# Three of seven quarter products with an operand's high and low parts side by side in one matmul

## The chip, the cores and the metric

The kernel runs on one core of one Trainium2 chip. The metric is device time in microseconds of one execution; lower is better. Before the change three runs took 1763.12 to 1763.74 us, median 1763.62. A core has a matrix engine (TensorE, PE in the profile; its weight loads are PEld), VectorE (DVE), ScalarE (ACT), GpSimd (POOL) and a queue engine (SP) that issues transfers. Matmul results land in PSUM, which this kernel uses as eight banks of 512 float32 columns.

## The reference

A decoder trunk of two layers over 512 tokens of width 1024, in float32. Each layer has a feed-forward block, a mixer, a second feed-forward block and a norm:

```python
h = x + 0.5 * swiglu(rms_norm(x, ffn1_norm[l]), ffn1_w1[l], ffn1_w3[l], ffn1_w2[l])
...
h = h + y @ w_out[l]          # y: convolution, sliding-window attention, memory attention
h = h + 0.5 * swiglu(rms_norm(h, ffn2_norm[l]), ffn2_w1[l], ffn2_w3[l], ffn2_w2[l])
x = rms_norm(h, final_norm[l])

def swiglu(x, w1, w3, w2):
    return (jax.nn.silu(x @ w1) * (x @ w3)) @ w2
```

The inner width is 2816, so 22 blocks of 128 columns of w1 and w3. The change is in the products with w1 and w3.

## The kernel before

**Precision.** A float32 operand is cut into a high part (ScalarE copies it to the matmul's rounded type) and a low part (VectorE subtracts the high part, L147). Three matmuls make one product: high x high, high weight x low data, low weight x high data (`mm3`, L178 to L180).

**Feed-forward.** `ffn` takes the first four of the 22 blocks plainly, as 512-column matmuls. The other 18 are taken in 9 pairs by `up_pair`. There each 2x2 product of halves (two blocks of weight columns by two halves of the 1024 channels, times two halves of the channels by two halves of the tokens) is formed from seven products of quarters instead of eight: sums and differences of weights (`wsum`, `raw`) times sums and differences of data. Each quarter product has 256 token columns and four blocks of 128 channels, so 12 matmuls. A pair does this for w1 (into `u`) and w3 (into `g`), 14 products in all, 168 matmuls.

**The data operands.** `Seven` holds the seven data operands as high and low parts: `first` makes those of products 1, 2 and 6 in the tiles `mh` and `ml`, `rest` those of 3, 5, 7 and 4 in `xhi` and `xlo`. Sums of quarters are VectorE adds (`msum`). They are made once per feed-forward block, while the four plain blocks and the first pairs run.

**Results.** Products accumulate in PSUM banks named after their pool: `po` (two), `pt` (two), `mm` (three) and `cf` (one). In a pair, products 1, 2, 6 and 5 used one `po` bank per weight (`xy`), 3, 7 and 4 one `pt` bank per weight (`zv`). ScalarE copies some results to SBUF (`part`), VectorE adds the rest (`add`, L386).

**Order.** The program is written once; a scheduler sets the order on each engine, and each engine then runs its own list in that order. The weight tiles `whi` and `wlo` have four buffers, `raw` and `aux` three. Each engine waits on semaphores at the head of its list, so whatever stands behind a waiting instruction waits too. The products with w2 (`begin` in `ffn`, 512 columns, `mm`) come after a group of pairs and may be mixed with its last products.

Of the kernel before, what the change touches and what calls it, by code (L numbers as in the profile page):

```python
# [11 lines left out]
F32R = mybir.dt.float32r  # L12
I32 = mybir.dt.int32
AF = mybir.ActivationFunctionType
ALU = mybir.AluOpType
AX = mybir.AxisListType
ALL = slice(None)

P = 128
D = 1024  # L20
S = 512
# [44 lines left out]
def trunk(ctx: ExitStack, tc: tile.TileContext, xT, memT, pos, w1a, w3a, w2a, w1b, w3b, w2b,  # L66
          wconv, wqk, wvm, wmem, wout, gains, small, rows, consts, out):
    nc = tc.nc
    V, G, A, T = nc.vector, nc.gpsimd, nc.scalar, nc.tensor

    const = ctx.enter_context(tc.tile_pool(name="const", bufs=1))
    res = ctx.enter_context(tc.tile_pool(name="res", bufs=1))
# [7 lines left out]
    turn, tail, hold = [0], [None], {}  # L80
# [10 lines left out]
    def bank(shape, tag):  # L91

        if tag == "mm":
            return ps_mm.tile(shape, F32, tag=tag, name=tag)
        return ps_ax.tile(shape, F32, tag=tag, name=tag, bufs=1 if tag == "cf" else 2)

    def tm(name, tag="t", bufs=None):
        return tmp.tile([P, S], F32, tag=tag, name=name, **({"bufs": bufs} if bufs else {}))
# [4 lines left out]
    def raw_tile(src, cols):  # L103
        raw = wst.tile([P, UNIT], F32, tag="raw", name="raw", bufs=3)
        nc.sync.dma_start(raw[:, 0:cols], src)
        return raw
# [5 lines left out]
    first = []  # L112
# [32 lines left out]
    def split(hi, lo, x, on):  # L145
        a = A.activation(hi, x, AF.Copy)  # L146
        return a, on.tensor_tensor(out=lo, in0=x, in1=hi.bitcast(F32), op=ALU.subtract)  # L147
# [29 lines left out]
    def mm3(ps, a, b, first, last, **more):  # L177
        T.matmul(ps, a[0], b[0], start=first, stop=False, **more)  # L178
        T.matmul(ps, a[0], b[1], start=False, stop=False, **more)  # L179
        tail[0] = T.matmul(ps, a[1], b[0], start=False, stop=last, **more)  # L180

    def at(p, *idx):
        return tuple(x[idx] for x in p)

    def blk(k, n=P):
        return slice(k * n, (k + 1) * n)
# [57 lines left out]
    class Stat:  # L244


        def __init__(self, tag, n=S, on=None):
            self.sums, self.tag, self.n, self.on = [], tag, n, on
# [18 lines left out]
    def operand():  # L267
        return (res.tile([P, KD, S], F32R, tag="xhi", name="xhi"), res.tile([P, KD, S], F32R, tag="xlo", name="xlo"))
# [16 lines left out]
    QT = 256  # L285
# [9 lines left out]
    class Seven:  # L295


        def __init__(self, n):
            self.n = n
            self.m = {}  # L300

        def quarter(self, half, i, t):

            return self.n[2 * half + i][:, :, blk(t, QT)]

        def first(self):
            near = (res.tile([P, 3, 4, QT], F32R, tag="nsh", name="mh"), res.tile([P, 3, 4, QT], F32R, tag="nsl", name="ml"))
            for i, j in enumerate((1, 2, 6)):
                self.m[j] = at(near, ALL, i)
            self.plain(1, 0, 0)  # L310
            self.plain(2, 1, 0)
            f = self.sum((0, 1), (1, 1), ALU.subtract)
            self.sum(f, (0, 0), ALU.subtract, f)
            self.cut(6, f)
# [7 lines left out]
            return out  # L322

        def plain(self, j, half, t):
            for i in range(2):
                hi, lo = at(self.m[j], ALL, blk(i, 2))
                split(hi, lo, self.quarter(half, i, t), V)

        def cut(self, j, f):
            hi, lo = (x.rearrange("p k t -> p (k t)") for x in self.m[j])  # L330
            split(hi, lo, f, V)

        def rest(self):
            far = tuple(x.rearrange("p k (u t) -> p (k u) t", t=QT) for x in operand())
            for i, j in enumerate((3, 5, 7, 4)):
                self.m[j] = at(far, ALL, blk(i, 4))
            self.plain(3, 1, 1)
            self.cut(5, self.sum((0, 0), (0, 1), ALU.subtract))
            f = self.sum((1, 1), (0, 1), ALU.subtract)
            self.cut(7, f)  # L340
            self.sum(f, (0, 0), ALU.add, f)
            self.sum(f, (1, 0), ALU.subtract, f)
            self.cut(4, f)
# [5 lines left out]
    def gated():  # L349
        p = gated_pair()  # L350
        return [at(p, ALL, i, ALL) for i in range(2)]

    def unit(x):
        p = pair()
        split(p[0], p[1], x, V)
        return p

    def up_pair(l, w13, f, M):

        raw = [raw_tile(w13[i][l, f], D) for i in range(2)]  # L360
        X = []
        for i in range(2):

            x = wst.tile([P, UNIT], F32, tag="aux", name="wsum", bufs=3)
            nc.sync.dma_start(x.rearrange("p (f c) -> p f c", f=2), w13[i][l, f : f + 2, :, 0:QW].rearrange("f p c -> p f c"))
            G.dma_start(x, w13[i][l, f + 1], accum_op=ALU.add)
            X.append(x)
        z = wst.tile([P, UNIT], F32, tag="raw", name="raw", bufs=3)
        for i in range(2):
            nc.sync.dma_start(z[:, blk(i, QW)], w13[i][l, f + 1, :, QW:])  # L370
        xy = [bank([P, S], "po") for _ in range(2)]
        zv = [bank([P, S], "pt") for _ in range(2)]
        x0, x1 = blk(0, QT), blk(1, QT)

        def product(ps, w, half, j, first=False):


            for k in range(4):
                mm3(ps, at(w, ALL, blk(4 * half + k)), at(M.m[j], ALL, k), first and k == 0, k == 3, skip_group_check=True)

        u, g = (tmp.tile([P, 2, S], F32, tag=t, name=t, bufs=n) for t, n in (("u", 1), ("g", 2)))
        part = [tm("part", "sq", 2) for _ in range(2)]
        to = (u, g)

        def add(out, a, b):
            V.tensor_tensor(out=out, in0=a, in1=b, op=ALU.add)  # L386

        for i in range(2):
            w = unit(raw[i])
            product(xy[i][:, x0], w, 0, 1, first=True)  # L390
            product(xy[i][:, x1], w, 1, 2)
            A.activation(part[i], xy[i], AF.Copy)
            add(to[i][:, 0, x0], part[i][:, x0], part[i][:, x1])

            add(raw[i][:, 0:QW], raw[i][:, 0:QW], X[i][:, QW:])
            add(raw[i][:, QW:], raw[i][:, QW:], raw[i][:, 0:QW])
        for i in range(2):
            w = unit(raw[i])
            product(xy[i][:, x0], w, 0, 6)
            A.activation(part[i][:, x1], xy[i][:, x0], AF.Copy)  # L400
            product(zv[i][:, x0], w, 1, 3, first=True)
        for i in range(2):
            w = unit(X[i])
            product(xy[i][:, x0], w, 1, 5)
            A.activation(part[i][:, x0], xy[i][:, x0], AF.Copy)
            product(zv[i][:, x1], w, 0, 7)
            add(to[i][:, :, x1], zv[i].rearrange("p (n t) -> p n t", n=2), part[i][:, x0].unsqueeze(1).to_broadcast([P, 2, QT]))
        w = unit(z)
        for i in range(2):
            product(zv[i][:, x1], w, i, 4)  # L410
            add(to[i][:, 1, x0], zv[i][:, x1], part[i][:, x1])
        out = gated()
        for n, sign in enumerate((1.0, -1.0)):
            A.activation(u[:, n], u[:, n], AF.Silu, scale=sign)
        M.gated = V.tensor_tensor(out=g, in0=g, in1=u, op=ALU.mult)
        for n, sign in enumerate((1.0, -1.0)):
            hi, lo = out[n]
            A.activation(hi, g[:, n], AF.Copy, scale=sign)
            V.scalar_tensor_tensor(out=lo, in0=g[:, n], scalar=sign, in1=hi.bitcast(F32), op0=ALU.mult, op1=ALU.subtract)
        return out  # L420

    def ffn(l, w13, w2, x, sums, factors, last, at_product, aside=None, closing=None):
# [55 lines left out]
        for q, (f0, nf) in enumerate(QUARTERS):  # L478
            ahead = 2 if q + 1 < len(QUARTERS) else 0
            for f in range(f0, f0 + nf + ahead, 2):  # L480
                if f not in g:
                    g[f], g[f + 1] = up_pair(l, w13, f, M)
                    if f == PLAIN:
                        with tc.issue_after(M.gated.ins):
                            rescale = after()
# [615 lines left out]
    for l in range(L):  # L1101
        x, new = nxt.x, Stat("st")
# [163 lines left out]
```

## Time and profile before

| | |
|---|---|
| three runs | 1763.12 to 1763.74 us, median 1763.62 |
| the profiled execution | 1764.53 us, its span 1762.8 us |
| granted TensorE clock | 0.998 |
| TensorE busy | 1746.5 us, 11004 matmuls |
| VectorE busy | 1281.3 us, 1898 instructions |
| ScalarE busy | 900.7 us, 1373 instructions |
| GpSimd busy | 195.6 us, 220 instructions |
| from HBM | 249.67 MB |

Times in the profile are microseconds from the start of the span. A timeline row is: start, duration, engine, line, operation, output<-inputs by the program's names, shapes; in square brackets the idle time just ahead of it and what ended that. Group rows have count, busy time, mean nanoseconds, idle time. Matmuls overlap, and their ends are modelled, so their starts tell more than their durations.

### The profile page before, as it was taken

How to read it: one execution, taken by the hardware profiler on the slowest of the kernel's cores; microseconds unless marked ns; L12 is line 12 of the kernel's file. 1: busy time of each engine (PE TensorE's matmuls, PEld its weight loads, DVE VectorE, ACT ScalarE, POOL GpSimd, SP SyncE). 2: the span in 40 equal slices, each digit the busy share in tenths (PEclk: the TensorE clock that was granted, in tenths of full speed). 3: DMA queues.
4: the chain of work that ended last, by engine and by line, in shares of the span. 5: the costliest groups of instructions: out<-in, count | busy, mean ns of one | idle time of the engine just before them, and what ended most of it. 6: DMA issues, size and time to landing. Idle time of an engine off the chain costs nothing.

```text
span 1762.8 us, 28084 instructions
## 1 busy us (share of the span) xinstructions
PE 1746.5 (99%) x11004; PEld 1576.7 (89%) x11004; DVE 1281.3 (73%) x1898; ACT 900.7 (51%) x1373; POOL 195.6 (11%) x220
## 2 busy tenths in 40 slices
PE   8999999999999999999999999999999999999998
PEld 7989999988888989898889898989888889998987
DVE  7968666589877757575677786666898677665756
ACT  6646444355765535353655463444467654353533
POOL 1001000006121000000010010000251310000000
PEclk9999999999999999999999999999999999999999
DMA  9456645257257546465567465642671766474622
GB/s 285 120 162 171 181 133 149 65 159 177 72 105 170 146 140 170 131 166 140 155 139 183 129 181 142 168 132 79 164 172 36 155 144 166 134 185 116 169 81 84
DMA packets 97205, 253.60 MB, mean 144 GB/s; under 512 B 9904, under 2 KB 16304, under 8 KB 97072
## 3 DMA queue, kind: packets, MB, share of 16 engines
q1 hardware_dynamic: 78064, 190.45, 35.4%
q0 software_dynamic: 19008, 61.35, 19.4%
q8 instruction: 86, 1.41, 0.3%
q14 instruction: 47, 0.39, 0.1%
HBM read 249.67 MB, written 2.10 MB: 143 GB/s over the span
## 4 chain that ended last, share of the span: by engine, by line
PE 98%; DVE 1%; DMA 1%; ACT 0%; issue 0%; SPq 0%; DVEq 0%; ACTq 0%
PE mm L178 14%; PE mm L179 14%; PE mm L180 14%; PE po L178 9%; PE po L179 9%; PE po L180 9%; PE pt L178 6%; PE pt L179 6%; PE pt L180 6%; PE po L870 2%; PE mm L818 1%; PE cf L178 1%; PE cf L180 1%; PE cf L179 1%; PE pt L859 1%; DMA raw<-in_w2b 1%
## 5 line engine op out<-in xcount | busy, mean ns | idle before, releaser
L146 ACT ACTIVATE whi<-raw 128x1024 fp32r<-128x1024 f32 (+3 forms) x346 | 326.2, 946 | 440.9 <-PE mm L179 219.9
L147 DVE TENSOR_TENSOR wlo<-raw,whi 128x1024 fp32r<-128x1024 f32 (+3 forms) x346 | 376.0, 1088 | 118.9 <-ACT whi L146 118.0
L179 PE MATMUL mm<-glo,whi 128*128 128x512 f32 (+1 forms) x752 | 292.1, 388 | 0.0
L178 PE MATMUL mm<-ghi,whi 128*128 128x512 f32 (+1 forms) x752 | 291.8, 390 | 0.0
L180 PE MATMUL mm<-ghi,wlo 128*128 128x512 f32 (+1 forms) x734 | 284.9, 388 | 0.0
L178 PE MATMUL pt<-xhi,whi 128*128 128x256 f32 x864 | 243.3, 283 | 1.4 <-DVE g L386 1.4
L180 PE MATMUL po<-mh,wlo 128*128 128x256 f32 x864 | 244.5, 283 | 0.0
L179 PE MATMUL po<-ml,whi 128*128 128x256 f32 x864 | 244.5, 283 | 0.0
L178 PE MATMUL po<-mh,whi 128*128 128x256 f32 x864 | 244.4, 283 | 0.0
L180 PE MATMUL pt<-xhi,wlo 128*128 128x256 f32 x864 | 243.9, 283 | 0.0
L179 PE MATMUL pt<-xlo,whi 128*128 128x256 f32 x864 | 243.9, 283 | 0.0
L506 DVE SCALAR_TENSOR_TENSOR h<-mm,h 128x512 f32<-128x512 f32 x126 | 86.3, 688 | 132.0 <-PE mm L180 131.9
L178 PEld LDWEIGHTS pt<-xhi,whi 128*128 128x128 f32 x864 | 165.2, 192 | 2.4 <-DVE g L386 1.6
L178 PEld LDWEIGHTS mm<-ghi,whi 128*128 128x128 f32 x752 | 141.4, 188 | 28.8 <-DVE h L506 1.2
L179 PEld LDWEIGHTS pt<-xlo,whi 128*128 128x128 f32 x864 | 165.7, 192 | 0.8
L178 PEld LDWEIGHTS po<-mh,whi 128*128 128x128 f32 x864 | 165.8, 192 | 0.7
L179 PEld LDWEIGHTS po<-ml,whi 128*128 128x128 f32 x864 | 165.8, 192 | 0.6
L179 PEld LDWEIGHTS mm<-glo,whi 128*128 128x128 f32 x752 | 141.3, 188 | 27.5
L180 PEld LDWEIGHTS po<-mh,wlo 128*128 128x128 f32 x864 | 165.8, 192 | 0.0
L180 PEld LDWEIGHTS pt<-xhi,wlo 128*128 128x128 f32 x864 | 165.7, 192 | 0.0
L180 PEld LDWEIGHTS mm<-ghi,wlo 128*128 128x128 f32 x734 | 137.8, 188 | 28.5
L1000 DVE SCALAR_TENSOR_TENSOR there<-ypad,par,there 128x512 f32<-128x512 f32 x180 | 136.0, 779 | 1.3
(334 smaller groups left out, 3322.0 us busy)
## 6 DMA issues: line engine op xcount, KB each, us to landing
raw<-in_w2a SPq DMA_DIRECT2D x48, 384.0 KB, 3.5
raw<-in_w2b SPq DMA_DIRECT2D x48, 384.0 KB, 3.6
raw<-in_w1b SPq DMA_DIRECT2D x26, 512.0 KB, 3.6
raw<-in_w3b SPq DMA_DIRECT2D x26, 512.0 KB, 3.7
raw<-in_w1a SPq DMA_DIRECT2D x25, 512.0 KB, 3.6
raw<-in_w3a SPq DMA_DIRECT2D x25, 512.0 KB, 4.0
wsum<-in_w1a SPq DMA_DIRECT2D x18, 512.0 KB, 4.4
wsum<-in_w3a SPq DMA_DIRECT2D x18, 512.0 KB, 4.3
```

The source lines that it names most:

```text
L146: a = A.activation(hi, x, AF.Copy)
L147: return a, on.tensor_tensor(out=lo, in0=x, in1=hi.bitcast(F32), op=ALU.subtract)
L178: T.matmul(ps, a[0], b[0], start=first, stop=False, **more)
L179: T.matmul(ps, a[0], b[1], start=False, stop=False, **more)
L180: tail[0] = T.matmul(ps, a[1], b[0], start=False, stop=last, **more)
L506: added = V.scalar_tensor_tensor(out=h[:, d, :], in0=ps, scalar=0.5, in1=h[:, d, :], op0=ALU.mult, op1=ALU.add)
L818: tail[0] = T.matmul(pp[i][:, z, :], q, k, start=not masked, stop=True, skip_group_check=True)
L859: tail[0] = T.transpose(pt[:, i, j, :], pr[:, i, blk(j)], ident)
L870: tail[0] = T.matmul(po[:, 2 * c + i, :], ptb[:, i, j, :], v, start=(j == 0), stop=(j == nk - 1))
L1000: V.scalar_tensor_tensor(out=cv[:, c, :], in0=ypad[:, c, j : j + S], scalar=conv_w[:, c, j : j + 1], in1=cv[:, c, :], op0=ALU.mult, op1=AL ...
```

## The change

An operand's high and low parts now lie beside each other, 256 columns each, for every block of channels. In products 2, 7 and 4 (`beside`) one matmul of 512 columns takes the high weight part times both, into the two halves of a bank; the low weight part times the high data part is added to the first half by a matmul of 256. The four wide ones of a product stand in a row, then the four narrow ones. VectorE sums the two halves (`summed`). Products 1, 6, 3 and 5 stay as they were. Product 1's accumulators (`x`, then used for 6 and 5) have a `pt` bank each; the results of 3 share the `cf` bank for both weights (`c`); each `beside` accumulator (`y`, `v`) takes a `po` bank, four in a pair.

```diff
         def first(self):
-            near = (res.tile([P, 3, 4, QT], F32R, tag="nsh", name="mh"), res.tile([P, 3, 4, QT], F32R, tag="nsl", name="ml"))
+            near = [res.tile([P, 6, 2, QT], F32R, tag=t, name=n) for t, n in (("nsh", "mh"), ("nsl", "ml"))]
             for i, j in enumerate((1, 2, 6)):
-                self.m[j] = at(near, ALL, i)
+                self.m[j] = [near[b // 6][:, b % 6] for b in range(4 * i, 4 * i + 4)]
...
         def rest(self):
-            far = tuple(x.rearrange("p k (u t) -> p (k u) t", t=QT) for x in operand())
+            far = [x.rearrange("p k (u t) -> p k u t", t=QT) for x in operand()]
             for i, j in enumerate((3, 5, 7, 4)):
-                self.m[j] = at(far, ALL, blk(i, 4))
+                z = self.whole[j] = far[i // 2][:, blk(i % 2, 4)]
+                self.m[j], self.ends[j] = [z[:, k] for k in range(4)], [z[:, 0:2], z[:, 2:4]]
...
-        xy = [bank([P, S], "po") for _ in range(2)]
-        zv = [bank([P, S], "pt") for _ in range(2)]
+        x = [bank([P, QT], "pt") for _ in range(2)]
...
+        def beside(ps, w, half, j, first=False):
+
+
+            def go(out, part, n):
+                for k in range(4):
+                    tail[0] = T.matmul(out, w[part][:, blk(4 * half + k)], M.m[j][k][:, 0:n], skip_group_check=True,
+                                       start=first and not part and k == 0, stop=part == 1 and k == 3)
+
+            go(ps, 0, 2)
+            go(ps[:, 0], 1, 1)
...
+        def summed(out, ps, a):
+            add(out, ps[:, 0], a)
+            add(out, out, ps[:, 1])
...
         for i in range(2):
             w = unit(raw[i])
-            product(xy[i][:, x0], w, 0, 1, first=True)
-            product(xy[i][:, x1], w, 1, 2)
-            A.activation(part[i], xy[i], AF.Copy)
-            add(to[i][:, 0, x0], part[i][:, x0], part[i][:, x1])
+            product(x[i], w, 0, 1, first=True)
+            A.activation(part[i][:, x0], x[i], AF.Copy)
+            y = bank([P, 2, QT], "po")
+            beside(y, w, 1, 2, first=True)
+            summed(to[i][:, 0, x0], y, part[i][:, x0])
...
+        c, v = bank([P, 2, QT], "cf"), []
         for i in range(2):
             w = unit(raw[i])
-            product(xy[i][:, x0], w, 0, 6)
-            A.activation(part[i][:, x1], xy[i][:, x0], AF.Copy)
-            product(zv[i][:, x0], w, 1, 3, first=True)
+            product(x[i], w, 0, 6)
+            A.activation(part[i][:, x1], x[i], AF.Copy)
+            product(c[:, i], w, 1, 3, first=not i)
         for i in range(2):
             w = unit(X[i])
-            product(xy[i][:, x0], w, 1, 5)
-            A.activation(part[i][:, x0], xy[i][:, x0], AF.Copy)
-            product(zv[i][:, x1], w, 0, 7)
-            add(to[i][:, :, x1], zv[i].rearrange("p (n t) -> p n t", n=2), part[i][:, x0].unsqueeze(1).to_broadcast([P, 2, QT]))
+            v.append(bank([P, 2, QT], "po"))
+            beside(v[i], w, 0, 7, first=True)
+            A.activation(to[i][:, 1, x1], v[i][:, 0], AF.Copy)
+            add(to[i][:, 1, x1], to[i][:, 1, x1], v[i][:, 1])
+            product(x[i], w, 1, 5)
+            A.activation(part[i][:, x0], x[i], AF.Copy)
+            add(to[i][:, 0, x1], c[:, i], part[i][:, x0])
+            add(to[i][:, 1, x1], to[i][:, 1, x1], part[i][:, x0])
         w = unit(z)
         for i in range(2):
-            product(zv[i][:, x1], w, i, 4)
-            add(to[i][:, 1, x0], zv[i][:, x1], part[i][:, x1])
+            beside(v[i], w, i, 4)
+            summed(to[i][:, 1, x0], v[i], part[i][:, x1])
```

The scheduler makes a new order of it. On TensorE, in the first pair of the first feed-forward block, this stands before the change where product 4 begins (`pt_531`, weights `whi_719`; `po_771` and `po_772` belong to products 1 of the next pair):

```order
L180 MATMUL po_771<-mh_337,wlo_780 128x256
L178 MATMUL po_772<-mh_337,whi_811 128x256
L179 MATMUL po_772<-ml_338,whi_811 128x256
L178 MATMUL pt_531<-xhi_494,whi_719 128x256
L180 MATMUL po_772<-mh_337,wlo_812 128x256
```

And this stands there now (`po_658` and `po_688` take products 7 and 4 of the first pair, for w1 and w3; `pt_761` is product 1 and `cf_826` product 3 of one pair and the next; line 388 is the matmul in `beside`):

```order
L180 MATMUL pt_761<-mh_337,wlo_797 128x256
L178 MATMUL cf_826<-xhi_494,whi_827 128x256
L179 MATMUL cf_826<-xhi_494,whi_827 128x256
L388 MATMUL po_658<-xlo_495,whi_714 128x512 x4
L388 MATMUL po_658<-xlo_495,wlo_715 128x256 x4
L388 MATMUL po_688<-xlo_495,whi_714 128x512 x4
L388 MATMUL po_688<-xlo_495,wlo_715 128x256 x4
```

Product 4 now comes as one row of four wide and four narrow matmuls per weight, and ahead of all of the next pair's product 2, whose bank is one of these two.

On VectorE, in the same place, this is the list before the change up to the low part of product 4's operand (the last row; `msum` is the operand, `u` and `g` the results of w1 and w3):

```order
L147 TENSOR_TENSOR wlo<-raw,whi 128x1024
L321 TENSOR_TENSOR msum<-msum,n 128x512 x2
L386 TENSOR_TENSOR raw<-raw,wsum 128x512
L386 TENSOR_TENSOR u<-pt,part 128x2x256
L321 TENSOR_TENSOR msum<-msum,n 128x512 x2
L147 TENSOR_TENSOR wlo<-raw,whi 128x1024
L386 TENSOR_TENSOR g<-pt,part 128x2x256
L386 TENSOR_TENSOR raw<-raw 128x512
L147 TENSOR_TENSOR xlo<-msum,xhi 128x1024
```

And now, from the second of these weight cuts on:

```order
L147 TENSOR_TENSOR wlo<-raw,whi 128x1024
L323 TENSOR_TENSOR msum<-msum,n 128x512 x2
L399 TENSOR_TENSOR u<-u,po 128x256
L399 TENSOR_TENSOR raw<-raw 128x512
L399 TENSOR_TENSOR g<-g,po 128x256
L399 TENSOR_TENSOR raw<-raw,wsum 128x512
L399 TENSOR_TENSOR u<-u,part 128x256
L147 TENSOR_TENSOR xlo<-msum,xlo 128x4x256
```

Between that weight cut and the operand's cut stand three adds of 256 columns, with results of products 7 and 5, and another operand sum; before there was one add of 512.

More of the change, by code (lines that the diff above doesn't have):

```diff
@@ L299, in __init__ @@
             self.n = n
-            self.m = {}
+            self.m, self.ends, self.whole = {}, {}, {}
         def quarter(self, half, i, t):
@@ L306, in first @@
         def first(self):
-            near = (res.tile([P, 3, 4, QT], F32R, tag="nsh", name="mh"), res.tile([P, 3, 4, QT], F32R, tag="nsl", name="ml"))
+            near = [res.tile([P, 6, 2, QT], F32R, tag=t, name=n) for t, n in (("nsh", "mh"), ("nsl", "ml"))]
             for i, j in enumerate((1, 2, 6)):
-                self.m[j] = at(near, ALL, i)
+                self.m[j] = [near[b // 6][:, b % 6] for b in range(4 * i, 4 * i + 4)]
+                self.ends[j] = [near[b // 6][:, b % 6 : b % 6 + 2] for b in (4 * i, 4 * i + 2)]
+            self.whole[6] = near[1][:, 2:6]
             self.plain(1, 0, 0)
@@ L324, in plain @@
         def plain(self, j, half, t):
-            for i in range(2):
-                hi, lo = at(self.m[j], ALL, blk(i, 2))
-                split(hi, lo, self.quarter(half, i, t), V)
+            for i, z in enumerate(self.ends[j]):
+                split(z[:, :, 0], z[:, :, 1], self.quarter(half, i, t), V)
         def cut(self, j, f):
-            hi, lo = (x.rearrange("p k t -> p (k t)") for x in self.m[j])
-            split(hi, lo, f, V)
+            z = self.whole[j]
+            split(z[:, :, 0], z[:, :, 1], f.rearrange("p (k t) -> p k t", k=4), V)
         def rest(self):
-            far = tuple(x.rearrange("p k (u t) -> p (k u) t", t=QT) for x in operand())
+            far = [x.rearrange("p k (u t) -> p k u t", t=QT) for x in operand()]
             for i, j in enumerate((3, 5, 7, 4)):
-                self.m[j] = at(far, ALL, blk(i, 4))
+                z = self.whole[j] = far[i // 2][:, blk(i % 2, 4)]
+                self.m[j], self.ends[j] = [z[:, k] for k in range(4)], [z[:, 0:2], z[:, 2:4]]
             self.plain(3, 1, 1)
@@ L378, in product @@
             for k in range(4):
-                mm3(ps, at(w, ALL, blk(4 * half + k)), at(M.m[j], ALL, k), first and k == 0, k == 3, skip_group_check=True)
+                m = M.m[j][k]
+                mm3(ps, at(w, ALL, blk(4 * half + k)), (m[:, 0], m[:, 1]), first and k == 0, k == 3, skip_group_check=True)
+        def beside(ps, w, half, j, first=False):
[5 more added lines that the diff above has]
+            go(ps[:, 0], 1, 1)
         u, g = (tmp.tile([P, 2, S], F32, tag=t, name=t, bufs=n) for t, n in (("u", 1), ("g", 2)))
```

## The prediction

> **What bounds the kernel now.** I read first the page's busy times and the chain that ended last, then who made TensorE wait, then the start times of single matmuls, and last the windows of the stretches in which VectorE has little room.
>
> ```profile
> PE 1746.5 (99%) x11004; PEld 1576.7 (89%) x11004; DVE 1281.3 (73%) x1898; ACT 900.7 (51%) x1373; POOL 195.6 (11%) x220
> PE 98%; DVE 1%; DMA 1%; ACT 0%; issue 0%; SPq 0%; DVEq 0%; ACTq 0%
> PE mm L178 <- ACT xhi L156: 6.0, 1, 6.0
> PE pt L178 <- DVE g L386: 1.4, 1, 1.4
> ```
>
> The chain of waits is TensorE's own queue for 98% of the span. The two long waits are 6.0 us once at the start and 1.4 us once in the last feed-forward block. So only two things can move the end: the time from one matmul to the next, and new waits on TensorE. The modelled duration of a matmul (283 ns in the groups) is no price, because matmuls overlap. The price is the distance between starts.
>
> ```profile
> 650.20:707.90 57.70, 57.70 (x482) 57.70 (x481) 40.58 (x50) 32.50 (x47) 5.18 (x6) 1.00 0.67 174
> 230.02 0.39 PE L178 MATMUL mm<-ghi,whi 128*128 128x512 f32 x1
> 232.74 0.28 PE L178 MATMUL po<-mh,whi 128*128 128x256 f32 x1
> ```
>
> The window (columns: length, then busy time and count of TensorE, its weight loads, VectorE, ScalarE, GpSimd, the granted clock) is one unbroken run of 256-column matmuls at full clock: 57.70 us / 482 = 120 ns each. Between the two other rows stand 12 matmuls of 512 columns: 2.72 us / 12 = 226.7 ns. Twice the columns cost 106.7 ns more, so each matmul carries about 13.3 ns whatever its width.
>
> **Term 1, fewer matmuls.** In products 2, 7 and 4 each block of 128 input channels had three matmuls of 256 columns, 360 ns. Now it has one of 512 and one of 256, 346.7 ns. Four feed-forward calls have 9 pairs each; a pair has six such products (4 is used twice per pair, once for either weight) of four blocks: 36 x 6 x 4 = 864 blocks, 864 x 13.3 ns = **-11.5 us**. TensorE's count should fall from 11004 to 10140. [...]
>
> **Term 2, changing width.** The four wide matmuls stand in a row among narrow ones, so I read what a change of width costs.
>
> ```profile
> 707.77 0.40 PE L178 MATMUL mm<-ghi,whi 128*128 128x512 f32 x1
> 708.47 0.28 PE L178 MATMUL pt<-xhi,whi 128*128 128x256 f32 x1
> 709.90 0.40 PE L178 MATMUL mm<-ghi,whi 128*128 128x512 f32 x1
> 713.40 0.40 PE L178 MATMUL mm<-ghi,whi 128*128 128x512 f32 x1
> 714.33 0.39 PE L179 MATMUL mm<-glo,whi 128*128 128x512 f32 x1
> ```
>
> The first four wide ones after narrow ones take 714.33 - 713.40 = 0.93 us instead of 0.907, 23 ns more. The twelve narrow ones from 708.47 to 709.90 take 1.43 us instead of 1.44, 10 ns less. Net 13 ns for each of 36 x 6 = 216 products: **+2.8 us**. Bounds: 0, since the three wide and twelve narrow ones from 707.77 to 709.90 take 2.13 us against 2.12 at the steady distances, and 216 x 23 ns = 5.0.
>
> **Term 3, more adds.** A result now lies in two halves of a bank that have to be summed. Per weight matrix and pair VectorE had three adds (256, 512 and 256 columns) after the products; it now has seven of 256.
>
> ```profile
> 74.14 0.68 DVE L386 TENSOR_TENSOR g<-pt,part 128x512 f32<-128x512 f32 x1
> 74.74 0.68 DVE L386 TENSOR_TENSOR raw<-raw 128x512 f32<-128x512 f32 x1
> 85.72 0.42 DVE L386 TENSOR_TENSOR g<-part 128x256 f32<-128x256 f32 x1
> 86.06 0.41 DVE L386 TENSOR_TENSOR u<-part 128x256 f32<-128x256 f32 x1
> L392 ACT ACTIVATE part<-po 128x512 f32<-128x512 f32 x72 | 41.8, 580 | 0.4 <-PE po L180 0.2
> L400 ACT ACTIVATE part<-po 128x256 f32<-128x256 f32 x72 | 27.3, 381 | 69.2 <-PE po L180 68.1 <-DVE u L386 0.8 <-DVE g L386 0.3
> ```
>
> One after another, 512 columns take 0.60 us and 256 take 0.34: 1.28 becomes 2.38, so 2.2 us more per pair and 79 us over 36 pairs; VectorE's busy time goes to about 1360 us. ScalarE trades one copy of 580 ns for two of 381, some 13 us in all, at 51% busy. In a steady run this is covered: the window at 650.20 has 40.58 us of VectorE work in 57.70 and 2.9 pairs, so 46.9 us after. If that cover were gone, 2.2 us per pair would land on TensorE. The cover is thin in two kinds of place.
>
> **Term 4, the start of each feed-forward block.** There VectorE also forms the operands of the seven products. The last one cut is that of product 4, whose low part is the `xlo<-msum` below; TensorE starts its first product at the PE rows.
>
> ```profile
> 54.73 0.28 PE L178 MATMUL po<-mh,whi 128*128 128x256 f32 x1
> 71.19 0.69 DVE L386 TENSOR_TENSOR u<-pt,part 128x512 f32<-128x512 f32 x1 [0.41 <-PE pt L180]
> 75.33 1.22 DVE L147 TENSOR_TENSOR xlo<-msum,xhi 128x1024 fp32r<-128x1024 f32 x1
> 78.00 0.28 PE L179 MATMUL pt<-xlo,whi 128*128 128x256 f32 x1
> 577.20 0.28 PE L178 MATMUL po<-mh,whi 128*128 128x256 f32 x1
> 597.13 1.21 DVE L147 TENSOR_TENSOR xlo<-msum,xhi 128x1024 fp32r<-128x1024 f32 x1
> 924.97 0.28 PE L178 MATMUL po<-mh,whi 128*128 128x256 f32 x1
> 945.58 1.21 DVE L147 TENSOR_TENSOR xlo<-msum,xhi 128x1024 fp32r<-128x1024 f32 x1
> 1447.83 0.28 PE L178 MATMUL po<-mh,whi 128*128 128x256 f32 x1
> 1467.76 1.21 DVE L147 TENSOR_TENSOR xlo<-msum,xhi 128x1024 fp32r<-128x1024 f32 x1
> ```
>
> Before, 194 narrow matmuls stand ahead of the one that needs it: 54.73 + 194 x 0.12 = 78.0, the row at 78.00. The cut ends at 76.55, so it is 1.45 us early. In the changed order only 138 narrow and 16 wide ones stand ahead, 20.19 us instead of 23.28: TensorE asks 3.09 us sooner, because product 4 now has to clear its two banks before the next pair may have them. On VectorE seven adds of 256 more and one of 512 fewer stand ahead of the cut: 7 x 0.34 - 0.60 = 1.78 us later. TensorE would wait 3.09 + 1.78 - 1.45 = 3.4 us. The same sum in the other blocks, whose margins are 2.14, 1.46 and 2.14 us, gives 2.7, 3.3 (one more add and four column turns stand ahead there) and 2.7: 12.2 us at most. Behind the waiting matmul stand all others, so it is paid in full. The lower bound is 0, if VectorE works off the adds in idle time such as the 0.41 us at 71.19. I take two thirds, nearer the upper end, as that row shows so little: **+8.2 us**.
>
> [...]
>
> **Term 5, layer 0's tables.** After its first two pairs VectorE also computes the rotary tables.
>
> ```profile
> 139.40:155.30 15.90, 15.86 (x36) 1.00 0.52 160
> 143.14 1.21 DVE L147 TENSOR_TENSOR wlo<-raw,whi 128x1024 fp32r<-128x1024 f32 x1
> 145.35 0.28 PE L180 MATMUL po<-mh,wlo 128*128 128x256 f32 x1
> 161.38 0.69 DVE L386 TENSOR_TENSOR raw<-raw,wsum 128x512 f32<-128x512 f32 x1 [3.18 <-issue]
> 181.42 0.69 DVE L386 TENSOR_TENSOR raw<-raw,wsum 128x512 f32<-128x512 f32 x1 [1.41 <-issue]
> ```
>
> VectorE is busy for 15.86 of 15.90 us. A weight cut ends at 144.35 and is used at 145.35: 1 us of margin. Three pairs stand here, 6.6 us of adds. The idle 3.18 and 1.41 us can take those of the later two; of the first pair's 2.2 about 1 is left after the margin: **+1.0 us**, bounds 0 and 5.
>
> The other edits I price at nothing. Product 1 gets its own banks, so ScalarE may copy its result while product 2 runs, but no row shows TensorE waiting for that copy. The new layout of high and low parts keeps the number and size of the cuts. No DMA is added or moved past another; the DMA issues keep their sizes.
>
> **Sum:** -11.5 + 2.8 + 8.2 + 1.0 = +0.5 us on the profiled execution's 1764.53. It stands 0.9 above the median of the runs, 1763.62, so I forecast **1764.1 us**: no change that can be measured. About 0.2% (3.5 us) is what a measurement here can tell from none.
>
> **The rivals.**
> - *VectorE makes up the adds and the gain arrives.* For it: VectorE has 27% of the span free, and before the change TensorE hardly ever waited for it. Against it: at 82 us a cut is only just ready (rows below: it ends at 82.40 and is used at 82.56). With some 2 us of waits in all: -11.5 + 2.8 + 2 = -6.7, so 1756.9; at best 1752.1.
>
> ```profile
> 81.18 1.22 DVE L147 TENSOR_TENSOR wlo<-raw,whi 128x1024 fp32r<-128x1024 f32 x1
> 82.56 0.28 PE L180 MATMUL pt<-xhi,wlo 128*128 128x256 f32 x1
> ```
>
> - *VectorE becomes the bound at the starts of the blocks: slower.* Place: the cut of product 4's operand, and layer 0's tables. Price: up to 12.2 + 5. It decides from 12.2 us of waits on, where the sum passes +3.5. At the upper ends -11.5 + 2.8 + 12.2 + 5 = +8.5, 1772; in the middle 1769.
> - *The wide matmul saves nothing.* If reading two operand parts in one go costs twice 120 ns, term 1 vanishes, term 2 with it, and terms 4 and 5 stay: +9.2, 1773. Against it: 226.7 ns in every long run of 512. [...]
>
> **Chances.** Forecast 0.42, gain arrives 0.30, VectorE bound 0.23, nothing saved 0.05. The forecast's own range is 1761 to 1767: nearly all within 0.2%, 0.02 to either side. The first rival is faster but for 0.01, the last two are slower. So faster 0.31, same 0.39, slower 0.30. The range reaches into both sides, 1756 to 1771, leaving about 0.1 out on each.
>
> **What would show it.** Term 1: 10140 matmuls, and 350 ns per block in a steady run. Term 2: a first distance of 233 to 236 ns in each row of four. Term 3: VectorE near 1360 us busy. Term 4: in the waits of TensorE, `po` at the new line of product 4 released by VectorE's cut (L147), four times, 2 to 3 us each; if it is missing, the first rival holds. Term 5: waits for weight cuts between 140 and 200 us. I am wrong if TensorE's waits stay under 5 us, if they grow in the steady runs too, or if wide matmuls lie apart by more than 230 ns on average.

## The result: 11.9 us slower, and the profile after

| | before | after |
|---|---|---|
| median of 6 runs | 1763.68 us (1763.12 to 1764.71) | 1775.61 us (1774.33 to 1777.82) |
| ratio to before | | 1.0068, 95% interval 1.0055 to 1.0081 |
| span of the profiled execution | 1762.8 us | 1774.9 us |
| granted TensorE clock | 0.998 | 0.995 |

The forecast was 1764.1, its range 1756 to 1771. The change makes the kernel slower, by more than the range allowed. The page of the changed kernel, busy times and chain of waits:

```profile
PE 1746.2 (98%) x10140; PEld 1532.7 (86%) x10140; DVE 1360.3 (77%) x2186; ACT 913.4 (51%) x1445; POOL 195.7 (11%) x220
PE 84%; DVE 7%; DMA 5%; issue 2%; ACT 1%; SPq 0%; DVEq 0%; POOLq 0%; ACTq 0%
```

The counts came as forecast: 10140 matmuls, VectorE 1360.3 us. The chain did not: it was TensorE's for 98%, now VectorE and transfers hold 12% of it. Who made TensorE wait, after the change (in total, times, longest):

```profile
PE cf L178 <- ACT whi L146: 4.9, 4, 1.8
PE po L388 <- DVE xlo L147: 3.2, 5, 0.8
PE cf L178 <- DVE g L399: 1.6, 3, 1.1
PE pt L180 <- DVE wlo L147: 1.1, 2, 0.6
PE cf L180 <- DVE wlo L147: 1.1, 1, 1.1
```

None of these stood in this view before. The view understates them, since a matmul's modelled end eats into the wait behind it: the longest, 1.8 us, is 1.95 by starts. So I worked from starts. For every matmul of 256 or 512 columns on all 128 rows I took the distance from its start to the next one and subtracted the steady distance of its width (120 or 226.7 ns). What is left is summed in two parts: distances over 60 ns too long are called **stalls** below, the rest is small change.

| us | before | after | difference |
|---|---|---|---|
| matmuls at their steady distance | 1601.6 | 1590.1 | -11.5 |
| small change | 1.6 | 3.9 | +2.3 |
| stalls | 12.3 | 33.5 | +21.2 |
| sum of the differences | | | +12.0 |

The spans differ by 12.1 us, so nothing is missing. The gain of the wide matmuls arrived in full, and stalls took it back nearly twice. Where the added stalls stand: starts of the four feed-forward blocks 6.9, 2.1, 4.4 and 2.1 us, 15.4 in all against 1.7 in the same stretches before; layer 0's tables 3.1; the plain matmuls ahead of the first pairs 1.3; a later pair of layer 1's first block 1.35; the rest, scattered, 1.8.

**The gain in a steady stretch.** TensorE's rows at the start of the second block, after its waits (x4: four matmuls in one row; the first number is the first one's start):

```profile
609.60 1.09 PE L388 MATMUL po<-xlo,whi 128*128 128x512 f32 x4
610.53 0.63 PE L388 MATMUL po<-xlo,wlo 128*128 128x256 f32 x4
611.00 0.28 PE L180 MATMUL cf<-xhi,wlo 128*128 128x256 f32 x1
```

From 609.60 to 610.53 four wide ones take 0.93 us, from 610.53 to 611.00 four narrow ones 0.47: 1.40 us for four blocks, 350 ns each instead of 360.

**The first block's start.** TensorE, then VectorE, then ScalarE of the changed kernel, in the stretch that the prediction's Term 4 speaks of:

```profile
70.95 1.17 PE L388 MATMUL po<-xlo,whi 128*128 128x512 f32 x4 [0.39 <-DVE xlo L147]
75.93 0.38 PE L180 MATMUL pt<-mh,wlo 128*128 128x256 f32 x1 [0.52 <-DVE wlo L147]
79.17 0.58 PE L178 MATMUL cf<-xhi,whi 128*128 128x256 f32 x1 [1.79 <-ACT whi L146]
80.47 2.08 PE L388 MATMUL po<-xlo,whi 128*128 128x512 f32 x4 [0.50 <-DVE xlo L147]
82.35 1.05 PE L388 MATMUL po<-xlo,wlo 128*128 128x256 f32 x4
```

```profile
69.59 1.21 DVE L147 TENSOR_TENSOR xlo<-msum,xlo 128x1024 fp32r<-128x1024 f32 x1
74.66 1.22 DVE L147 TENSOR_TENSOR wlo<-raw,whi 128x1024 fp32r<-128x1024 f32 x1
75.80 1.28 DVE L323 TENSOR_TENSOR msum<-msum,n 128x512 f32<-128x512 f32 x2
77.00 0.41 DVE L399 TENSOR_TENSOR u<-u,po 128x256 f32<-128x256 f32 x1
77.33 0.68 DVE L399 TENSOR_TENSOR raw<-raw 128x512 f32<-128x512 f32 x1
77.94 0.41 DVE L399 TENSOR_TENSOR g<-g,po 128x256 f32<-128x256 f32 x1
78.27 0.68 DVE L399 TENSOR_TENSOR raw<-raw,wsum 128x512 f32<-128x512 f32 x1
78.87 0.41 DVE L399 TENSOR_TENSOR u<-u,part 128x256 f32<-128x256 f32 x1
79.20 1.22 DVE L147 TENSOR_TENSOR xlo<-msum,xlo 128x1024 fp32r<-128x1024 f32 x1
```

```profile
78.08 1.04 ACT L146 ACTIVATE whi<-raw 128x1024 fp32r<-128x1024 f32 x1
```

VectorE has no idle time from 61.65 to 82.50: none of its rows there carries a bracket. So whatever is added ahead of an item on its list makes that item late. The low part of product 4's operand (`xlo`, last VectorE row) ends at 80.42, where it ended at 76.55 before. The stalls of the first, second, third and fourth PE row are 0.55, 0.68, 1.95 and 0.80 us. Only the last is for product 4's cut. The first is for the cut of product 7 at 69.59, and the longest, at 79.17, is for a high weight part (ScalarE's row at 78.08) whose input is the `raw` that VectorE adds up at 77.33: the weight sum of the next pair's product 3. All four wait for VectorE's list.

Not all of that lateness comes from the adds. VectorE begins the block's normalised input `n` here, before the change and after it:

```profile
29.99 5.39 DVE L292 SCALAR_TENSOR_TENSOR n<-h,gn,R 128x512 f32<-128x512 f32 x8
32.63 5.39 DVE L292 SCALAR_TENSOR_TENSOR n<-h,gn,R 128x512 f32<-128x512 f32 x8
```

It is 2.6 us later, after a weight cut that waited for ScalarE's copy, which had waited 2.75 us for a transfer. TensorE's first product of the block starts only 1.1 us later (55.86 in place of 54.73). So some 1.5 us of this start's waits were there before the first added add.

**Half a clock.** Those four stalls sum to 4.0 us; the start's total is 6.85. Most of the rest stands from the last two PE rows on: from 80.47 to 82.35 the four wide matmuls take 1.88 us, where they took 0.93 above. Windows around the first and the third start (length, busy time and count of TensorE, weight loads, VectorE, ScalarE, GpSimd, then the granted clock):

```profile
75.00:79.00 4.00, 1.86 (x14) 1.45 (x12) 4.00 (x8) 2.27 (x3) 0.00 (x0) 0.97 0.73 152
78.76:85.59 6.83, 5.92 (x18) 4.85 (x19) 4.58 (x8) 1.82 (x4) 0.00 (x0) 0.50 0.21 58
85.59:89.00 3.41, 3.41 (x27) 3.24 (x27) 3.08 (x4) 1.64 (x3) 0.00 (x0) 1.00 0.03 8
955.00:959.00 4.00, 1.73 (x11) 1.27 (x10) 4.00 (x8) 2.05 (x2) 0.00 (x0) 1.00 0.23 45
959.40:962.81 3.41, 3.41 (x13) 2.92 (x12) 1.69 (x3) 1.28 (x3) 0.00 (x0) 0.50 0.37 115
```

The clock is granted at 0.50 from 78.76, inside the longest wait, to 85.59, and from 959.40, behind the third start's two waits, to 962.81. A wait is also followed by a distance that is about 0.1 us too long, at full clock too (0.10 and 0.11 us at the second start). Without the waits and these, 2.5 us are left of the 6.85 at the first start and 1.5 of the 4.4 at the third: the clock cost **4.0 us** that no wait shows.

**A later wait.** In layer 1's first block VectorE itself stands idle ahead of a weight sum, and an add of results is queued behind:

```profile
1061.68 0.41 DVE L399 TENSOR_TENSOR g<-g,po 128x256 f32<-128x256 f32 x1
1065.51 0.69 DVE L399 TENSOR_TENSOR raw<-raw,wsum 128x512 f32<-128x512 f32 x1 [3.41 <-issue]
1067.25 0.42 DVE L399 TENSOR_TENSOR g<-cf,part 128x256 f32<-128x256 f32 x1
```

The bank `cf` is given back by the add at 1067.25, and TensorE's matmul into it starts 1.25 us late, at 1067.7. What VectorE waited for is a transfer, the part of the weight sum `wsum` that GpSimd adds in:

```profile
1057.12 0.86 POOL L368 DMA_DIRECT2D wsum<-in_w3a  x1 [17.76 <-DMA wsum<-in_w3a]
```

It is issued here and lands at 1065.43 by the trace's record of landings, just ahead of the add at 1065.51. The kernel before waited 1.30 us for the same transfer at this place. So this stall is not VectorE being short of time.

### The profile page after: what moved, and what is told of

It is laid out like the page before. It is cut to its first block, busy times and chain, and to the rows that moved or that the text cites. A ratio compares the mean times of both kernels' runs of the same rounds, so it can differ in the third digit from the quotient of the medians.

```text
span 1774.9 us, 26623 instructions
## 1 busy us (share of the span) xinstructions
PE 1746.2 (98%) x10140; PEld 1532.7 (86%) x10140; DVE 1360.3 (77%) x2186; ACT 913.4 (51%) x1445; POOL 195.7 (11%) x220
## 4 chain that ended last, share of the span: by engine, by line
PE 84%; DVE 7%; DMA 5%; issue 2%; ACT 1%; SPq 0%; DVEq 0%; POOLq 0%; ACTq 0%
PE po L388 14%; PE mm L178 13%; PE mm L179 13%; PE mm L180 13%; PE pt L178 5%; PE pt L180 5%; PE pt L179 5%; PE cf L178 2%; PE cf L180 2%; PE cf L179 2%; DMA wsum<-in_w3a 2%; DVE wlo L147 2%; DMA wsum<-in_w3b 2%; PE po L893 2%; PE po L178 1%
## 5 line engine op out<-in xcount | busy, mean ns | idle before, releaser
L388 PE MATMUL po<-xlo,whi 128*128 128x512 f32 x576 | 160.3, 400 | 3.6 <-DVE xlo L147 3.2
L388 PEld LDWEIGHTS po<-xlo,whi 128*128 128x128 f32 x576 | 101.6, 192 | 19.5 <-DVE xlo L147 3.7
L178 PE MATMUL mm<-xhi,whi 128*128 128x512 f32 x272 | 108.5, 403 | 6.6 <-ACT xhi L156 6.1
L180 PE MATMUL mm<-xhi,wlo 128*128 128x512 f32 x272 | 106.8, 392 | 0.3 <-DMA wlo<-in_w1a 0.3
L179 PE MATMUL mm<-xlo,whi 128*128 128x512 f32 x272 | 106.6, 392 | 0.0
L388 PEld LDWEIGHTS po<-xlo,wlo 128*128 128x128 f32 x576 | 89.9, 192 | 12.6
L178 PE MATMUL cf<-xhi,whi 128*128 128x256 f32 (+1 forms) x304 | 88.8, 292 | 6.6 <-ACT whi L146 4.9
L388 PE MATMUL po<-xlo,wlo 128*128 128x256 f32 x576 | 92.8, 283 | 0.0
L180 PE MATMUL cf<-xhi,wlo 128*128 128x256 f32 (+1 forms) x304 | 87.9, 289 | 1.1 <-DVE wlo L147 1.1
L147 DVE TENSOR_TENSOR wlo<-wsum,whi 128x1024 fp32r<-128x1024 f32 x72 | 87.7, 1218 | 0.0
```

The costliest lines, as they stand in the source:

```text
L388: tail[0] = T.matmul(out, w[part][:, blk(4 * half + k)], M.m[j][k][:, 0:n], skip_group_check=True, start=first and not part and k == 0, st ...
```

## The experiments

Two theories. **V**: the added adds make VectorE late with cuts and weight sums where it has no room, and TensorE waits for those. **B**: the new banks, `cf` above all (one bank, given back late), and the order that they force hold TensorE up. All stalls below are worked out as above (12.3 us before, 33.5 after). Verdicts go by the medians; stalls come from one profiled execution each and tell the places. One execution lies up to 2.4 us off its median (e1).

| run | median, us | ratio to before, 95% | stalls | matmul time to before |
|---|---|---|---|---|
| e1 second adds left out | 1765.19 | 1.0007 (0.9998 to 1.0017) | 19.3 | -11.5 |
| e2 new banks, narrow matmuls | 1767.69 | 1.0027 (1.0017 to 1.0038) | 16.7 | 0 |
| e3 before, more VectorE work | 1768.84 | 1.0032 (1.0020 to 1.0043) | 17.9 | 0 |
| e4 wide from the third pair on | 1766.15 | 1.0020 (1.0010 to 1.0030) | 23.2 | -8.9 |
| e5 product 3 copied out | 1773.84 | 1.0056 (1.0043 to 1.0068) | 31.3 | -11.5 |
| e8 first two pairs as before | 1762.81 | 1.0000 (0.9991 to 1.0009) | 16.5 | -8.9 |
| e9 and those at the tables | 1759.99 | 0.9980 (0.9971 to 0.9989) | 13.7 | -8.0 |
| e10 as e9, product 3 not copied | 1760.37 | 0.9983 (0.9974 to 0.9992) | 12.8 | -8.0 |
| e11 as e9, only the first pair | 1760.74 | 0.9987 (0.9978 to 0.9995) | 15.7 | -8.9 |

**e1, the second adds left out.** Against the changed kernel:

```diff
         def summed(out, ps, a):
             add(out, ps[:, 0], a)
-            add(out, out, ps[:, 1])
...
             A.activation(to[i][:, 1, x1], v[i][:, 0], AF.Copy)
-            add(to[i][:, 1, x1], to[i][:, 1, x1], v[i][:, 1])
```

> The changed kernel without the second add of each wide product: the low half of the data operand's share is left out of the result of products 2, 7 and 4, so the output is not the reference's; matmuls, banks and copies are those of the change. VectorE has 4 adds of 256 per weight and pair instead of 7. Theory V (the added adds make VectorE late with the cuts, and the waits bring the half clock): TensorE's stalls fall from 33 us back to about 14, so 1764 - 11.5 + 2.3 + 2 = about 1756 us. Rival B (the new banks and the order that they force cause the waits): the adds do not matter, 1772 us or more.

Measured 1765.19, 10.4 us less than after. Its page and its waits:

```profile
PE 1740.8 (99%) x10140; PEld 1530.8 (87%) x10140; DVE 1287.0 (73%) x1970; ACT 914.7 (52%) x1445; POOL 195.0 (11%) x220
```

```profile
PE cf L178 <- DVE g L399: 2.8, 2, 1.8
PE cf L178 <- ACT whi L146: 2.3, 4, 1.1
PE po L388 <- DVE xlo L147: 0.3, 2, 0.2
```

VectorE is 73.3 us less busy, with 216 adds fewer, and 14.1 us of stalls go with them: two thirds of what the change added in these two executions, and by the medians, 10.4 us apart, about half. (The late start of `n` above, some 1.5 us of the changed kernel's stalls, is missing in e1's execution too: 29.86.) Product 4's operand is ready about as early as before. Its cut ends 21.8, 21.1, 22.2 and 21.1 us after the first narrow matmul of the four blocks; before the change it was 21.8, 21.1, 21.8 and 21.1, after it 24.6, 22.1, 23.8 and 22.1. The wait for operand cuts nearly vanishes (3.2 to 0.3), the clock holds through the starts (1.00), and layer 0's tables cost nothing. That is V's mechanism. But the time lies between the forecasts, 9 us over V's and 7 under B's, and 7.1 us of stalls more than before remain with VectorE hardly busier than then. Of these, 3.4 stand at the starts, where TensorE still asks sooner, and 3.6 in layer 1's first block at `cf`, behind late `wsum` transfers (VectorE idle for 3.70 us ahead of the weight sum at 1030.45 and 4.53 us ahead of the one at 1052.49). So V is not all.

**e2, the new banks with narrow matmuls.** The changed kernel with the layout, banks and order of products, but twelve narrow matmuls for products 2, 7 and 4, and so no second add:

```diff
-            go(ps, 0, 2)
-            go(ps[:, 0], 1, 1)
+            product(ps[:, 0], w, half, j, first)
```

> The changed kernel's layout and banks, but products 2, 7 and 4 as twelve narrow matmuls into one half of their bank, and one add each. Theory V: the adds are as many as before (4 of 256 against 2 of 256 and one of 512), so TensorE hardly waits: 1764 us, within 3. Rival B: the banks are those of the change, so its 21 us of new stalls stay without the gain of the wide matmuls: 1775 to 1785 us.

Measured 1767.69, 4.4 us over before (1763.26 in this comparison): just above V's range and well under B's. Its waits:

```profile
PE cf L178 <- DVE g L398: 2.0, 2, 1.1
PE po L178 <- ACT xlo L146: 1.3, 1, 1.3
```

So the banks and the order that follows from them have a price of their own, and part of it is at `cf`, as B has it. But it falls in the same places: 4.0 us at the four starts (1.7 before the change), and 1.3 more than before at the tables and 1.2 in layer 1's first block.

**e3, more VectorE work in the kernel before.** Each pair gets seven more VectorE operations of 256 columns on its results, a maximum of a value with itself, which changes nothing in them:

```diff
+        def more(a):
+            V.tensor_tensor(out=a, in0=a, in1=a, op=ALU.max)
...
             add(to[i][:, 0, x0], part[i][:, x0], part[i][:, x1])
+            more(to[i][:, 0, x0])
```

> The kernel before, with seven more VectorE operations of 256 columns per pair (the maximum of a result with itself, in place, which changes nothing): 2.4 us of VectorE per pair, as the change adds 2.2; matmuls and banks as before. Theory V: TensorE waits at the starts of the blocks and at layer 0's tables, 10 to 20 us in all: 1772 to 1784 us. Rival B: 1764 to 1767 us.

Measured 1768.84, 5.6 us over before, with no wide matmul and no new bank. That is between the two forecasts.

```profile
PE 1748.2 (99%) x11004; PEld 1577.1 (89%) x11004; DVE 1367.0 (77%) x2150; ACT 899.9 (51%) x1373; POOL 195.9 (11%) x220
```

```profile
PE pt L178 <- DVE u L386: 2.6, 2, 2.1
PE pt L179 <- DVE xlo L147: 2.5, 2, 1.5
```

VectorE is as busy as after the change (1367.0 and 1360.3 us), and the very wait of Term 4 appears in the old kernel: product 4 for `xlo`. Stalls: 4.5 us at the starts (1.7 before), and 2.6 more than before at the tables. With e1 and e2 this gives a rough sum of the 21.2 us. Banks and order alone add 4.4 us of stalls (e2), with the wide matmuls 7.1 (e1), the adds alone 5.6 (e3): 12.7. The half clock has 4.0 more. The last 4.5 us come only when all stand together. That each then spends slack which the others needed is likely, but no run shows it by itself.

**e4, wide only from the third pair on.** The changed kernel; the first two pairs of each block keep its banks, but have narrow matmuls and one add:

```diff
+        wide = f >= WIDE
...
+            if not wide:
+                return product(ps[:, 0], w, half, j, first)
...
+            if wide:
+                add(out, out, ps[:, 1])
```

> The change in the last seven of nine pairs of each feed-forward block; the first two pairs take narrow matmuls and one add, in the new banks. Theory V: the waits at the four starts (some 14 us with the half clock) go, 7/9 of 9.2 us is gained, layer 0's tables (3 us) and waits in the steady runs (3 us) stay: 1764 - 7.2 + 6 = 1763 us. Rival B: the banks are new in all pairs, so the starts stay slow: 1772 us or more.

Measured 1766.15, 9.5 us less than after and 3 over V's 1763. The starts fall from 15.4 to 3.9 us and the clock holds (1.00 there), but the tables keep 3.3 and layer 1's first block 3.3:

```profile
PE cf L179 <- DVE g L404: 2.5, 2, 2.3
PE po L179 <- ACT xlo L147: 1.1, 1, 1.1
```

So the starts are the main place, with the new banks still there. Whether the rest is the banks or VectorE is for the next runs.

**e5, product 3's results copied out of `cf` early.** The changed kernel, with the add made free of the bank:

```diff
             product(c[:, i], w, 1, 3, first=not i)
+        for i in range(2):
+            A.activation(to[i][:, 0, x1], c[:, i], AF.Copy)
...
-            add(to[i][:, 0, x1], c[:, i], part[i][:, x0])
+            add(to[i][:, 0, x1], to[i][:, 0, x1], part[i][:, x0])
```

> The changed kernel with one thing altered: ScalarE copies both halves of product 3's results from the bank cf into the result tile as soon as both are there, and the add after product 5 works on that copy. The bank cf is then free some 5 us earlier in each pair, and no longer waits for VectorE. Theory B (the new banks and the order they force, cf above all, since it alone has a single bank and is given back by a late add): the waits on cf that VectorE ends vanish, and with them 3 to 6 us of stalls; about 1771 us. Theory V (the adds make VectorE late with cuts): the cuts are as late as before and the four starts keep their 15 us of stalls; 1774 to 1776, with ScalarE busier by 72 x 0.58 = 42 us.

Measured 1773.84. Its waits:

```profile
PE cf L178 <- ACT whi L146: 5.2, 4, 2.1
PE po L388 <- DVE xlo L147: 3.0, 5, 0.8
```

The waits on `cf` that VectorE ended are gone, as B said, and outside the starts this execution has 4.5 us of stalls less than the changed kernel's. At the starts the waits for weights and for product 4's cut stand about as they were, and the stalls rose from 15.4 to 17.7 us, because the clock was now halved at three of them and not at two (mean granted clock 0.994, in the changed kernel 0.995). So the medians differ by 1.8 us only, with ranges that just overlap. V's 1774 was the nearer forecast, but it came by a gain away from the starts and a loss of clock, and the price of `cf` in the changed kernel is not measured by this run alone.

**e8 and e9, the old path where VectorE has no room.** e8 is e5 with a choice per pair: the first two pairs of each block (`f` 4 and 6) go as before the change, banks, matmuls and adds. e9 adds layer 0's next three pairs, those at the rotary tables:

```diff
-        if f < 8:
+        if f < 8 or f < 14 and l == 0 and w13[0] is w1a:
             xy = [bank([P, S], "po") for _ in range(2)]
             zv = [bank([P, S], "pt") for _ in range(2)]
...
         else:
             x = [bank([P, QT], "pt") for _ in range(2)]
```

> The kernel of the run before this one, but the first two pairs of each of the four feed-forward blocks go wholly as in the kernel before the change: its banks, narrow matmuls, three adds. Seven of nine pairs keep the wide matmuls and the added adds: 4 x 7 x 6 x 4 = 672 blocks x 13.3 ns = -8.9 us of matmul time, change of width about +1.8. Theory V (the stalls are the late cuts at the starts): the 15 us there fall to the 1.7 of before, layer 0's tables keep about 3; the time comes to about 1763.7 - 8.9 + 1.8 + 4 = 1760. Theory B (banks delay the pairs everywhere): the steady runs keep 3 to 5 us, 1763 to 1765. If stalls only move to where the new path begins, 1766 or more.

> As the run before this one, and in layer 0's first block the pairs that run while VectorE computes the rotary tables go as before the change too. They give up 3 pairs x 24 blocks x 13.3 ns = 1.0 us of matmul time and about 0.2 of width changes. Theory V: the 3 us of stalls at the tables go as well, about 1758. If the stalls at the tables do not come from the adds, nothing but the 0.8 us is seen: 1761.

Measured 1762.81 and 1759.99. Stalls at the starts fall to 0.9 us in e8 (0.78 in the first block, 0.08 in the third, none in the others), and at the tables they go from 2.5 in e8 to 0 in e9: each goes where the old path was put. Since that path brings back the old banks together with the old adds, this shows the place and does not tell V from B. What is left at e9's starts, 2.1 us, is no more than a wait for the last adds of a pair, which the kernel before has too (1.7). The waits of e9:

```profile
PE pt L178 <- DVE g L398: 1.4, 2, 0.8
PE cf L180 <- DVE wlo L147: 0.4, 1, 0.4
```

Both medians came 2 to 3 us above what V gave (1760 and 1758), e8's at the edge of B's 1763 to 1765; in the later pairs of the second and third blocks its execution keeps 3.0 us of added stalls, as B has it. On the other hand, the profiled spans, 1759.8 and 1757.8, lie 3.0 and 5.0 us under the 1762.8 of before, near V's 3.7 and 5.7. Which of the two is V's miss is not settled; e8's runs scatter by more (1760.39 to 1768.99). e9 beats both kernels: 0.9980, interval 0.9971 to 0.9989.

**e10 and e11, what e9 needs.** e10 takes e5's copy out of e9 again; e11 leaves only one pair per block on the old path, outside layer 0's first:

```diff
-        if f < 8 or f < 14 and l == 0 and w13[0] is w1a:
+        if f < 6 or f < 14 and l == 0 and w13[0] is w1a:
```

> The best kernel so far (first two pairs, and layer 0's pairs at the tables, as before the change) without ScalarE's early copy of product 3's results: the bank cf is again given back by VectorE's add after product 5, as in the changed kernel. Theory B (the single bank cf holds TensorE up in the steady runs): 1 to 2 us of waits on cf come back, about 1761.5. Theory V (only the starts and the tables are short of VectorE): no difference that can be measured, 1759 to 1760.5.

> The best kernel so far, but in the later three blocks only the first pair goes as before the change, the second one wide. Three more pairs with wide matmuls: 3 x 24 x 13.3 ns = -1.0 us, some +0.2 for the change of width. Theory V with the place I gave it (the cut of product 4's operand, which stands behind the adds of the first pair's products and is needed in the second): the second pair may be wide only if VectorE has caught up by then; it was busy without a gap until the second pair's product 3, so 1 to 2 us of waits per block come back: 1762 to 1764. If the cut of product 4 alone was the trouble, the wait is gone with the first pair: about 1759.

Measured 1760.37 and 1760.74, e9's time within the uncertainty. Waits of e10, then of e11:

```profile
PE cf L178 <- DVE g L398: 1.1, 2, 0.9
```

```profile
PE pt L179 <- DVE xlo L147: 1.6, 3, 0.6
```

In e10 the single bank `cf`, given back by VectorE as in the change, costs two waits of 1.1 us in all and no measurable time, as V had it: in the steady runs of this kernel `cf` is not what holds TensorE up. In e11 product 4's cut is late again, three times and 1.6 us in all, where V gave 1 to 2 us per block and 1762 to 1764: with the first pair's adds out of the way most of the lateness goes. The other case in the expectation, no wait at all and 1759, did not come either; the time lies between the two.

## Why the prediction was wrong, step by step

- **Term 1 (-11.5) was right.** 10140 matmuls, -11.5 us at the steady distances, and 350 ns per block in the rows shown.
- **Term 2 (+2.8) was right:** +2.3, and 0.93 us for a row of four.
- **Term 3 was right in its size** (1360.3 us) and nearly in its cover: outside the starts and the tables 4.4 us of stalls were added, 1.3 of them ahead of the first pairs and 1.35 in layer 1's first block, where VectorE waits for a transfer. The sum had none of these.
- **Term 4 (+8.2) is the step that failed.** Place and mechanism were right: four starts, VectorE's cuts late, TensorE asking sooner. e1 takes most of it away by the adds, e4 and e8 by the place. The size failed twice. First, "I take two thirds", on the ground that VectorE could work off the adds in idle time. In the second and fourth blocks that was about right: the cut came 1.0 us later, where the sum had about 1.8, and the waits there are 1.8 us each in place of 2.7. In the first and third they are 4.0 and 2.6 where the sum had 3.4 and 3.3 at most; in the first VectorE had no idle row from 61.65 to 82.50, and some 1.5 us of lateness were there before. With the 0.1 us behind each wait the stalls at the starts, less the clock's share, are 11.4 us (15.4 - 4.0), 3.2 over the term and within its upper bound of 12.2. Second, the term priced waits only, and the waits cost clock: 4.0 us, in no bound of the prediction. A wait of 1.7 us in the old last block went away. 11.4 + 4.0 - 1.7 = +13.7 in place of +8.2. The sign that the prediction named came four times, but with 0.5 to 0.8 us each and not 2 to 3: the weight sum for product 3 stands ahead on TensorE's list and took 4.9 us of the waits. That the waits still came within the term's bounds is in part luck.
- **Term 5 (+1.0) was too small:** +3.1, inside its bounds of 0 to 5. They vanish without the second adds (e1) and with the old path there (e9).
- **The sum:** -0.5 (Term 2), +5.5 (Term 4), +2.1 (Term 5) and +4.4 (elsewhere) are the 11.5 us by which the span's +12.1 passes the sum's +0.5, to within 0.1.
- **The rivals.** "VectorE becomes the bound at the starts" happened; it had 0.23 and 1769 to 1772, short by the clock and by the stalls elsewhere. The list of what would make me wrong held: the waits grew past the starts.
- **PSUM banks.** Stalls stand at all four starts (6.9, 2.1, 4.4 and 2.1 us). Freeing the one single bank, `cf` (e5), left them, 17.7 us in all, and taking VectorE's adds away (e1) brought the starts from 15.4 us to 5.1. So `cf` is not what holds TensorE up there; no run gave the other pools more banks.

## What to carry to other kernels

A change that takes time off the bounding engine and puts work on a helper has to be costed in the stretches where the helper has no idle row: there every added microsecond, and every microsecond by which the bound asks sooner, can become a wait. Here the stalls at the starts came to 11.4 us of an upper bound of 12.2, so a share of the bound was too little. Use the new form where the helper has room and keep the old one where it has not: 36 pairs changed gave +11.9 us, 25 of them -3.5 (e9; -3.1 without its early copy). And price a cluster of stalls on TensorE by more than its length, since the clock behind it can be halved: here it stood at 0.50 for 6.83 and for 3.41 us and cost 4.0 us.

## What the runs showed of the hardware

The granted clock fell to half at stalls that were short. After the change it happened inside a wait of 1.79 us and behind waits of 1.52 and 0.76 us, and lasted 6.83 and 3.41 us. It is not a matter of the wait's length alone. The third block's start in the changed kernel, then in e5, then two windows of e5, of its third and its second start:

```profile
957.30 0.39 PE L178 MATMUL cf<-xhi,whi 128*128 128x256 f32 x1 [1.52 <-ACT whi L146]
958.56 1.39 PE L388 MATMUL po<-xlo,whi 128*128 128x512 f32 x4 [0.76 <-DVE xlo L147]
```

```profile
956.74 0.39 PE L178 MATMUL cf<-xhi,whi 128*128 128x256 f32 x1 [1.51 <-ACT whi L146]
958.00 1.19 PE L388 MATMUL po<-xlo,whi 128*128 128x512 f32 x4 [0.76 <-DVE xlo L147]
```

```profile
956.60:962.00 5.40, 4.51 (x28) 3.96 (x29) 4.35 (x7) 1.86 (x4) 0.00 (x0) 1.00 0.24 67
608.03:611.44 3.41, 3.41 (x12) 2.84 (x12) 2.13 (x4) 1.10 (x3) 0.00 (x0) 0.50 0.32 85
```

The same two waits, 1.5 and 0.76 us, cost the clock in one (0.50) and not in the other (1.00). At the second start it is the other way round: waits of 0.78 and 0.75 us halved it in e5, and 0.77 and 0.76 us left it at 1.00 in the changed kernel. Within a run, the changes in the trace's clock records between 50 and 1500 us lie whole multiples of 3.413 us apart: 873.81 us in the changed kernel, from 85.59 to 959.40, is 256 of them, and 522.24 us in e5 is 153. The longest single wait at a place where the clock fell was 2.13 us (in e5's first block; in the list above as 2.1). What exactly halves the clock stays open: no run varied the length of a stall, or its place between such points, by itself.
